# Hybrid trunk on one core: late transfers planned to land later, and a retry, in the kernel's own orderer

## The chip, the cores and the metric

The kernel runs on one core of a Trainium2 chip. The time is the device time of one execution in microseconds; the runs of before gave 1721.27, 1724.09 and 1725.7, median 1724.09. The engines are PE (TensorE; PEld its weight loads), DVE (VectorE), ACT (ScalarE), POOL (GpSimd) and SP (SyncE). Each takes its instructions in the order of its own queue and waits on semaphores. DMA transfers are issued by SP (all loads of weights and tiles, and the last outputs) and by POOL (most stores).

## What is computed

One layer of a hybrid trunk for two request groups, 1024 prompt tokens and 8 x 16 sample tokens, with shared weights, all in float32. Cut to what matters:

```python
mod = silu(c) @ w_ada + b_ada
shift, scale, gate = split(mod[:, None, :], 3)
h = rms_norm(x, norm_g) * (1 + scale) + shift
q, k, v, z_att, z_ssd, xbc, dt_raw, gates = split(h @ w_in, IN_SPLITS)
q, k = rms_norm(q, q_norm_g), rms_norm(k, k_norm_g)          # per head
o_att, k_st, v_st = attn_fn(q, k, v)                          # own chunk + 8 chunks before
att_branch = (o_att * silu(z_att)) @ w_att_proj
xbc, conv_new = causal_dwconv(xbc, conv_buf, conv_w, conv_b)
xs, bm, cm = split(silu(xbc))
dt, a = softplus(dt_raw + dt_bias), -exp(a_log)
y, h_new = ssd_scan(xs, dt, a, bm, cm, h0)                    # chunked scan of 32 heads
y = rms_norm((y + d_skip * xs) * silu(z_ssd), ssd_norm_g)     # in 4 groups
ssd_branch = y @ w_ssd_proj
g_att, g_ssd = split(gates)
out = x + gate * ((sigmoid(g_att) * att_branch + sigmoid(g_ssd) * ssd_branch) @ w_out)
```

D_MODEL is 1024, there are 16 attention heads of 64, the SSD width is 2048 with a state of 128, and 1152 = 1024 + 128 tokens go through the dense layers together. Outputs are `out` and the new keys, values, convolution rows and scan states of both groups.

## The kernel before

`trunk_kernel` lays the work out feature-major: a tile holds 128 features by 1152 tokens (`NT`), in one SBUF area (`arena`, with slots per stage). A dense product in float32 is made of three float16 products: each weight block and operand is split into a high and a low part, and PE adds high x high, high x low and low x high in PSUM (L970, L971, L973 in `dense`, on 384 tokens at a time; L876, L877, L878 in `quad_dense`, on 288).

*Stages.* Attention of the eight head pairs comes first (to about 600 us of the trace). Then come the 16 pairs of SSD heads: a `dense` product for z (evicted at L1985 and L1986), convolution and scan (`ssd`, L2013 and L2113 among its lines, its result written to `y_d` in DRAM), with gate columns in between (`gate_dense`, evicted by ACT's tanh at L1919 and stored by POOL at L1920). From about 1300 us on come the quarter-product stages, all through `quad_dense`: the rest of the gates, the attention projection, the two halves of the SSD projection and the output projection. There a block product is done with seven quarter products instead of eight, from sums and differences of quarters. The sums of the weights are made on DVE by `quad_sums` in the SSD stage and written to `sum_d` in DRAM (POOL, L712), and loaded again later.

*Weights.* `w_ahead` (L679, SP) loads raw weights up to three buffers ahead. `w_split` or `quad_split` splits them: L697 on ACT makes the high part, L698 on DVE the low part; L689 on ACT takes the sum of squares of weights (1024 or 512 wide) and of operands (576 wide) that a later test of the ranges needs.

*Operands of the quarter products.* `differences` (L2209 to L2212, DVE) and `halved` (L2198 ACT, L2200 DVE) split them, `h_pieces` (L2245) and `ssd_prep` (L2281 loads `y_d`, L2286 scales it) feed them. Both are waited for by PE.

*Evictions in `quad_dense`.* `kept` copies the first of a pair of PSUM banks to SBUF (L895, ACT), `joined` adds a second one on DVE (L901). PSUM has three banks of a kind "d", three of a kind "g" and one double one of a kind "s" (the names of PE's outputs begin with these letters), so the eviction of one product frees the bank of a later one. L1108 are four small products for the modulation, which read what L2381 (`mod_gate`, ACT) copied out of PSUM.

*The order.* The program is first recorded in an order in which the generators of the stages take turns. Then `Order` makes the order of every queue anew. `build` forms units: an instruction each, but on PE up to three matmuls of one kind and one output together ("packed"), and any number of small ones; it finds what depends on what by the regions that are read and written, and by the PSUM banks. `run` is a list scheduler with a model of the durations (`cost`): it takes the engine that can go on first, and on it, of the units that are ready by its clock, the earliest in recorded order, with units first whose inputs are there with a margin (`SAFE`: 1000 ns behind PE, 300 behind DVE and ACT, 2500 behind a DMA). The margin decides only among units that are ready; a unit is ready when its inputs' planned ends have passed. For a DMA the planned end comes from eight lanes and one shared bus in `run`. `apply` then chains each engine's instructions in the planned order. Nothing is planned at run time; the real waits are semaphores.

If a test at the end finds a value out of range, a second block of the program (`general_kernel`) computes all again; with these inputs it doesn't run.

## Time and profile before

| | before |
|---|---|
| runs, us | 1721.27, 1724.09, 1725.7; median 1724.09 |
| profiled execution, us | 1723.17 |
| its span, first to last instruction, us | 1721.4 |
| mean granted TensorE clock | 0.998 |
| PE idle from 0 to 600 us, us | 13.18 |
| PE idle from 600 to 1300 us, us | 9.46 |
| PE idle from 1300 to 1700 us, us | 13.52 |
| PE idle from 1700 us to the end, us | 6.64 |

How to read the rows below. In the table of busy times, the number behind the engine is its busy time in microseconds, its share of the span, and the count of instructions. A row of the waits names the waiting engine with its output and line, then the engine, tile and line that ended the wait, then the total, the times and the longest. A row of a timeline has the start and the length in microseconds, the engine, line and operation, what it writes and reads, and in square brackets how long the engine had been idle and who ended that. Matmuls are pipelined: one of 384 columns lasts about 0.33 us, and the next starts about 0.16 us behind it. A row of a chain has the start, the length and what it is. A row of stretches has the stretch, its length, the busy time of PE, PEld, DVE, ACT and POOL with the number of instructions, the granted clock, the share of the DMA engines and GB/s.

### The profile page before, as it was taken

The page shows a single profiled execution, that of the slowest core. Times are in us where ns is not written, and L with a number is a line of the kernel's source. Part 1 is how long each engine was busy: PE and PEld are TensorE (multiplying, and loading weights), DVE is VectorE, ACT ScalarE, POOL GpSimd, SP SyncE. Part 2 cuts the span into 40 slices and gives each one's busy share as a digit, 9 for nine tenths or more (in the row PEclk, how much of TensorE's full clock was granted, in tenths as well). Part 3 has the DMA queues.
Part 4 walks back from the last instruction along what each step waited for, and adds up shares of the span by engine and source line. Part 5 has one row for each costly group of instructions (what it writes and reads, how often), then busy time and mean ns, then how long its engine had stood idle before and what let it go on. Part 6 is the DMA issues. An engine that isn't in the chain of part 4 may idle for free. (4 is left out here: it accounts for less than half of the span.)

```text
span 1721.4 us, 36659 instructions
## 1 busy us (share of the span) xinstructions
PE 1678.6 (98%) x14265; PEld 1120.4 (65%) x14265; DVE 1376.6 (80%) x2539; ACT 1058.1 (61%) x2123; POOL 369.1 (21%) x640
## 2 busy tenths in 40 slices
PE   7999999999999999999999999999999999999998
PEld 3556565556565556666666666666657777777776
DVE  6458767878877888889988998997798677888973
ACT  8766556566565668457655765665379665774550
POOL 0133233135133111322321232232212101010000
PEclk9999999999999999999999999999999999999999
DMA  9248789797978687676858867788756866687661
GB/s 383 82 122 210 170 228 225 168 232 187 219 219 192 165 199 221 181 221 199 194 172 263 241 194 238 235 216 268 284 198 221 274 240 234 232 287 264 224 212 65
DMA packets 299249, 369.16 MB, mean 214 GB/s; under 512 B 211692, under 2 KB 213368, under 8 KB 299064
## 3 DMA queue, kind: packets, MB, share of 16 engines
q1 hardware_dynamic: 282040, 307.65, 64.0%
q0 software_dynamic: 17024, 59.06, 9.3%
q8 instruction: 114, 1.87, 0.5%
q14 instruction: 71, 0.58, 0.1%
HBM read 244.08 MB, written 74.06 MB: 185 GB/s over the span
## 5 line engine op out<-in xcount | busy, mean ns | idle before, releaser
L970 PE MATMUL d<-arena 128*128 128x384 f16 x1320 | 432.0, 327 | 4.4 <-DVE arena L1986 2.0
L973 PE MATMUL d<-arena 128*128 128x384 f16 x1320 | 431.5, 327 | 1.2 <-DVE arena L698 1.2
L971 PE MATMUL d<-arena 128*128 128x384 f16 x1320 | 431.3, 327 | 0.0
L689 ACT ACTIVATE arena<-arena 128x1024 bf16<-128x1024 f32 (+4 forms) x217 | 199.2, 918 | 130.1 <-DMA arena<-in_wall_dram 88.2
L698 DVE SCALAR_TENSOR_TENSOR arena<-arena 128x1024 f16<-128x1024 f32 (+2 forms) x157 | 181.8, 1166 | 61.0 <-ACT arena L697 60.5
L697 ACT ACTIVATE arena<-arena 128x1024 f16<-128x1024 f32 (+2 forms) x157 | 155.4, 994 | 83.2 <-DMA arena<-sum_d 40.5
L970 PEld LDWEIGHTS <-arena 128*128 128x128 f16 x1320 | 129.2, 98 | 90.9 <-issue 12.1
L1023 PE MATMUL d<-arena 128*128 128x384 f16 (+1 forms) x568 | 187.0, 329 | 0.0
L1024 PE MATMUL d<-arena 128*128 128x384 f16 (+1 forms) x568 | 186.3, 328 | 0.0
L1025 PE MATMUL d<-arena 128*128 128x384 f16 (+1 forms) x568 | 186.2, 328 | 0.0
L973 PEld LDWEIGHTS <-arena 128*128 128x128 f16 x1320 | 129.0, 98 | 87.8 <-DVE arena L698 1.9
L971 PEld LDWEIGHTS <-arena 128*128 128x128 f16 x1320 | 129.1, 98 | 82.5 <-issue 5.8
L1569 ACT ACTIVATE arena<-arena 128x640 f32<-128x640 f32 (+4 forms) x144 | 100.8, 701 | 63.4 <-DVE arena L1572 63.0
L877 PEld LDWEIGHTS <-arena 128*128 128x128 f16 x1120 | 109.3, 98 | 39.7 <-issue 12.2
L878 PEld LDWEIGHTS <-arena 128*128 128x128 f16 x1120 | 109.3, 98 | 32.4 <-issue 4.3
L876 PEld LDWEIGHTS <-arena 128*128 128x128 f16 x1120 | 109.4, 98 | 29.3 <-issue 1.5
L876 PE MATMUL d<-arena 128*128 128x288 f16 x400 | 114.5, 286 | 5.9 <-DVE arena L901 3.9
L876 PE MATMUL g<-arena 128*128 128x288 f16 x400 | 114.5, 286 | 1.2 <-DVE arena L901 1.2
L877 PE MATMUL g<-arena 128*128 128x288 f16 x400 | 114.5, 286 | 1.2 <-DVE arena L2200 1.2
L877 PE MATMUL d<-arena 128*128 128x288 f16 x400 | 114.5, 286 | 0.2 <-DVE arena L2200 0.2
L878 PE MATMUL g<-arena 128*128 128x288 f16 x400 | 114.5, 286 | 0.0
L878 PE MATMUL d<-arena 128*128 128x288 f16 x400 | 114.5, 286 | 0.0
(277 smaller groups left out, 3521.8 us busy)
## 6 DMA issues: line engine op xcount, KB each, us to landing
arena<-in_quad_dram SPq DMA_DIRECT2D x80, 512.0 KB, 7.0
arena<-in_wall_dram SPq DMA_DIRECT2D x77, 512.0 KB, 5.2
sum_d<-arena POOLq DMA_DIRECT2D x40, 512.0 KB, 4.9
arena<-sum_d SPq DMA_DIRECT2D x40, 512.0 KB, 4.9
arena<-acs_d SPq DMA_DIRECT2D x32, 576.0 KB, 6.2
arena<-in_kc_dram SPq DMA_DIRECT2D x64, 256.0 KB, 4.4
arena<-in_vc_dram SPq DMA_DIRECT2D x64, 256.0 KB, 3.6
arena<-in_wada_dram SPq DMA_DIRECT2D x24, 512.0 KB, 3.7
```

The source lines that it names most:

```text
L689: keep(nc.scalar.activation(junk[:, :n], x, AF.Square, scale=scale * n ** -0.5, accum_out=sums[:, c:c + 1]))
L697: keep(nc.scalar.activation(hi, x, AF.Copy, scale=scale))
L698: keep(nc.vector.scalar_tensor_tensor(lo, x, scale, hi, ALU.mult, ALU.subtract))
L876: nc.tensor.matmul(ps, wh, xh[:, c], start=first and k == 0, stop=False, skip_group_check=not first)
L877: nc.tensor.matmul(ps, wh, xl[:, c], start=False, stop=False, skip_group_check=not first)
L878: nc.tensor.matmul(ps, wl, xh[:, c], start=False, stop=k == 3, skip_group_check=not first)
L970: nc.tensor.matmul(ps, hi.r[:, wc], kh.r[:, tok], start=k == 0, stop=False)
L971: nc.tensor.matmul(ps, hi.r[:, wc], kl.r[:, tok], start=False, stop=False)
L973: nc.tensor.matmul(ps, lo.r[:, wc], kh.r[:, tok], start=False, stop=k == nk - 1)
L1023: nc.tensor.matmul(ps, kh.r[:, tok], wh, start=k == 0, stop=False)
L1024: nc.tensor.matmul(ps, kh.r[:, tok], wl, start=False, stop=False)
L1025: nc.tensor.matmul(ps, kl.r[:, tok], wh, start=False, stop=k == KT - 1)
```

## The change

Two things. First, if `run` finds no unit that can go on, it no longer stops with an error: it raises `Stuck` with the names of the matmuls that are ready, these are put into a set `apart`, and `build` and `run` are done again with each of them opening a unit of its own. Second, in `run`, a DMA whose planned start is behind 600,000 ns of the planner's clock counts as landed 1000 ns later for everything that reads it. The lanes and the bus go on as before.

```diff
+class Stuck(Exception):
+    pass
...
-        self.pinned, self.cuts = pinned, cuts
+        self.pinned, self.cuts, self.apart = pinned, cuts, set()
...
-                if last and last["key"] == key and x.name not in self.cuts and (small or len(last["ins"]) < 3):
+                if last and last["key"] == key and x.name not in self.cuts and x.name not in self.apart and (small or len(last["ins"]) < 3):
...
-            assert best, ("no unit can go on", [(e, [(u["i"], u["ins"][0].name) for u in ready[e]][:4]) for e in engines])
+            if not best:
+                raise Stuck([x.name for u in ready["PE"] for x in u["ins"]])
...
                 lanes[e][k] = bus + 700
-                lat = bus + 700 - t
+                lat = bus + 700 - t + (1000.0 if t > 600000.0 else 0.0)
...
     order = Order(tc, list(nc.cur_bb.bb.instructions), pinned, cuts, slow, fill, fast)
-    order.build()
-    order.run()
+    while True:
+        order.build()
+        try:
+            order.run()
+            break
+        except Stuck as x:
+            assert not order.apart.issuperset(x.args[0]), "no unit can go on"
+            order.apart.update(x.args[0])
     order.apply()
```

In the built program `apart` stays empty, so the units are those of before. The order is not. It is the same up to about 603 us of the trace of before, and from there on rows change places on all five queues. Three places follow; the lines of the changed kernel are five higher (L1919 is L1924, and so on), and the number behind a name is that of the buffer.

The first is POOL and ACT where the last sum of weights (`sum19_d`) is stored and the modulation is taken out of PSUM (`g664`), from 1244 to 1264 us of the trace. POOL before:

```order
L1920 DMA gate_d_79<-arena_73 128x384
L712 DMA sum19_d_101<-arena_73 256x1x512
L2074 DMA out_hp_dram<-arena_73 128x128
L712 DMA sum19_d_101<-arena_73 256x1x512
L1920 DMA gate_d_79<-arena_73 128x384 x3
L2125 DMA y_d_76<-arena_73 128x1152
```

and now:

```order
L1925 DMA gate_d_79<-arena_73 128x384
L717 DMA sum19_d_101<-arena_73 256x1x512
L2079 DMA out_hp_dram<-arena_73 128x128
L1925 DMA gate_d_79<-arena_73 128x384
L717 DMA sum19_d_101<-arena_73 256x1x512
L1925 DMA gate_d_79<-arena_73 128x384
L2130 DMA y_d_76<-arena_73 128x1152
```

One gate store has moved ahead of the second sum store. ACT at the same time, before:

```order
L1919 ACTIVATE arena_73<-d656_14235 128x384
L689 ACTIVATE arena_73<-arena_73 128x576 x2
L2198 ACTIVATE arena_73<-arena_73 128x1152
L1919 ACTIVATE arena_73<-d660_14325 128x384
L697 ACTIVATE arena_73<-arena_73 128x1024
L2198 ACTIVATE arena_73<-arena_73 128x1152
L689 ACTIVATE arena_73<-arena_73 128x576 x4
L2381 ACTIVATE arena_73<-g664_14407 128x512
```

and now:

```order
L1924 ACTIVATE arena_73<-d656_14235 128x384
L1924 ACTIVATE arena_73<-d660_14325 128x384
L702 ACTIVATE arena_73<-arena_73 128x1024
L694 ACTIVATE arena_73<-arena_73 128x576 x2
L2131 ACTIVATE arena_73<-arena_73 128x1152
L2203 ACTIVATE arena_73<-arena_73 128x1152
L2386 ACTIVATE arena_73<-g664_14407 128x512
L1924 ACTIVATE arena_73<-d663_14371 128x384
L2203 ACTIVATE arena_73<-arena_73 128x1152
L694 ACTIVATE arena_73<-arena_73 128x576 x4
```

An eviction and a weight split have moved ahead of the first two L689, and L2381 ahead of one L2198 and four L689; one L2126 has come forward.

The second is PE, where it reads what L2381 made (`g665`). Before:

```order
L971 MATMUL d666_14428<-arena_73 128x384
L973 LDWEIGHTS arena_73
L973 MATMUL d666_14428<-arena_73 128x384
L1108 MATMUL g665_14408<-arena_73 128x9 x4
L970 LDWEIGHTS arena_73
L970 MATMUL d667_14472<-arena_73 128x384
```

and now:

```order
L976 MATMUL d666_14428<-arena_73 128x384
L978 LDWEIGHTS arena_73
L978 MATMUL d666_14428<-arena_73 128x384
L1113 MATMUL g665_14408<-arena_73 128x9 x4
L975 LDWEIGHTS arena_73
L975 MATMUL d666_14428<-arena_73 128x384
```

The four L1108 stood behind the last of the matmuls of `d666`; now twelve matmuls of `d666` stand behind them.

The third is ACT from 1521 to 1530 us, in the SSD projection, around the evictions of `d739` to `g742`. Before:

```order
L697 ACTIVATE arena_73<-arena_73 128x512
L2198 ACTIVATE arena_73<-arena_73 128x1152
L697 ACTIVATE arena_73<-arena_73 128x1024 x2
L689 ACTIVATE arena_73<-arena_73 128x1024
L895 ACTIVATE arena_73<-d739_17160 128x288
L895 ACTIVATE arena_73<-d740_17161 128x288
L689 ACTIVATE arena_73<-arena_73 128x1024
L895 ACTIVATE arena_73<-g741_17162 128x288
L895 ACTIVATE arena_73<-g742_17163 128x288
```

and now:

```order
L2203 ACTIVATE arena_73<-arena_73 128x1152 x2
L900 ACTIVATE arena_73<-d739_17160 128x288
L900 ACTIVATE arena_73<-d740_17161 128x288
L702 ACTIVATE arena_73<-arena_73 128x512
L702 ACTIVATE arena_73<-arena_73 128x1024
L900 ACTIVATE arena_73<-g741_17162 128x288
L900 ACTIVATE arena_73<-g742_17163 128x288
L702 ACTIVATE arena_73<-arena_73 128x1024
L694 ACTIVATE arena_73<-arena_73 128x1024 x2
```

The evictions of `d739` and `d740` have moved ahead of three weight splits, those of `g741` and `g742` ahead of one split and two L689.

## The prediction

> **What bounds the kernel now.** I read the page's busy table first, then the busy time of the engines by stretch, then the waits of PE behind 600 us, then the timeline of PE at each wait and of the engine that it waits for. Line numbers are those of before; in the changed kernel a line of `trunk_kernel` stands five higher.

> ```profile
> span 1721.4 us, 36659 instructions
> PE 1678.6 (98%) x14265; PEld 1120.4 (65%) x14265; DVE 1376.6 (80%) x2539; ACT 1058.1 (61%) x2123; POOL 369.1 (21%) x640
> ```

> PE is busy nearly throughout, so an order of the same instructions can win only what PE waits. How much of that lies where the order changes (from 603 us on) is read from the stretches. The second column is the length, the third PE's busy time, then PE weight loads, DVE, ACT, POOL.

> ```profile
> 600.00:1300.00 700.00, 690.54 (x5480) 455.47 (x5478) 617.72 (x974) 433.90 (x809) 169.85 (x276) 1.00 0.75 219
> 1300.00:1700.00 400.00, 386.48 (x3137) 305.82 (x3136) 313.23 (x440) 248.21 (x446) 28.35 (x53) 1.00 0.69 235
> ```

> PE's idle time is 9.46 us in the first stretch and 13.52 us in the second: 22.98 us, 1.3% of the span, is all that can be won by ending waits. The waits by who ends them (total, times, longest) show many short ones and one of 3.1 us:

> ```profile
> PE d L876 <- DVE arena L901: 3.9, 4, 1.5
> PE g L1108 <- ACT arena L2381: 3.1, 1, 3.1
> PE d L970 <- DVE arena L1986: 2.0, 1, 2.0
> PE d L973 <- DVE arena L698: 1.2, 2, 0.7
> ```

> The producers are PSUM evictions and small results (L901, L895, L1919, L2381, L2198/L2200). In the timelines below they are ready in time, but stand on ACT or DVE behind an instruction that waits for a DMA. Those queues go in order, so a late transfer holds back work that has nothing to do with it.

> **The change, part by part.** *The taking apart:* in the built program no unit is taken apart; the orderer finds an order at the first try. It costs and gives nothing. *The added microsecond:* no instruction is added or removed. What waits for a transfer is planned 1 us later, so other work is put ahead of it. Counted in the two orders, 594 of DVE's and 567 of ACT's rows stand elsewhere, nearly always by a few rows. PE's 12,785 matmuls are the same; 1,151 of them move, by 99 places at most. Seven places carry the sum.

> (1) Near 1209 us.

> ```profile
> 1208.46 1.04 ACT L697 ACTIVATE arena<-arena 128x1024 f16<-128x1024 f32 x1
> 1209.93 0.32 PE L970 MATMUL d<-arena 128*128 128x384 f16 x1 [1.03 <-ACT arena L1919]
> ```

> PE waits 1.03 us for an eviction that ACT runs behind a weight split of 1.04 us. Now the eviction stands first: **0.95 us** won (0.9 to 1.03).

> (2) The wait at 1260 us. Times and lengths of the matmuls, the chain, ACT, and POOL with its median store (the last number):

> ```profile
> 1258.69 0.33 PE L970 MATMUL d<-arena 128*128 128x384 f16 x1
> ...
> 1260.48 0.33 PE L973 MATMUL d<-arena 128*128 128x384 f16 x1
> 1263.88 1.06 PE L1108 MATMUL g<-arena 128*128 128x9 f32 x8 [3.08 <-ACT arena L2381]
> ...
> 1265.13 0.53 PE L973 MATMUL d<-arena 128*128 128x384 f16 x1
> ...
> 1268.33 0.42 PE L970 MATMUL d<-arena 128*128 128x384 f16 x1
> ```
> ```profile
> 1244.98 7.54 DMA sum_d<-arena
> ...
> 1252.62 1.36 DVE arena L2245
> ```
> ```profile
> 1247.02 0.47 ACT L1919 ACTIVATE arena<-d 128x384 f32<-128x384 f32 x1
> 1254.06 0.69 ACT L689 ACTIVATE arena<-arena 128x576 bf16<-128x576 f32 x1 [6.56 <-issue]
> ...
> 1255.55 1.15 ACT L2198 ACTIVATE arena<-arena 128x1152 f16<-128x1152 f32 x1
> ...
> 1263.25 0.58 ACT L2381 ACTIVATE arena<-g 128x512 f32<-128x512 f32 x1
> ```
> ```profile
> 1247.79 0.56 POOL L1920 DMA_DIRECT2D gate_d<-arena  x1 [2.09 <-ACT arena L1919]
> ```
> ```profile
> sum_d<-arena POOLq DMA_DIRECT2D x40, 512.0 KB, 4.9
> ```

> The second sum store took 7.54 us; DVE's L2245 waited for it, ACT's L689 for L2245, and L2381 came out behind that backlog at 1263.83. Two things move. POOL now issues a gate store ahead of the sum store, and that gate store waits for ACT's L1919, which ends at 1247.49; so the sum store goes out where that issue of 0.56 us ends, near 1248.4, and lands 4.9 (the median row) to 7.54 us later, at 1253.3 to 1255.9. And ACT runs L1919 and L697 in its idle 6.56 us, then two L689, one L2126, one L2198 and L2381, the other L2198 and four L689 behind it. Counted from the landing: L2245 1.36, two L689 1.49 (from 1254.06 to the next row's 1255.55), L2126 and L2198 1.1 each, L2381 0.58, together 5.6: L2381 ends at 1258.9 to 1261.5. But PE has its four L1108 (eight records) twelve matmuls earlier, from 1258.69 on instead of 1260.64. The wait becomes 0.2 to 2.8 us: 0.3 to 2.9 won, and I take **1.5**, the middle, since nothing says which store length comes.

> Behind that wait the matmuls start 0.32 us apart instead of 0.16: from 1265.13 to 1268.33 ten take 3.20 us where the same spacing as at 1258.69 to 1260.48 (1.79 us for eleven) gives 1.63, and the clock says the same:

> ```profile
> 1265.00:1268.60 3.60, 3.60 (x14) 1.75 (x13) 3.60 (x5) 3.60 (x6) 0.58 (x2) 0.53 0.84 267
> ...
> 900.00:903.00 3.00, 1.87 (x11) 0.96 (x11) 3.00 (x4) 0.00 (x0) 0.00 (x0) 1.00 1.07 317
> ```

> 3.60 x (1 - 0.53) = **1.7 us** lost. The second row is behind the 2.0 us wait for L1986, and there the clock stays at 1.00. So the point lies between 2.0 and 3.08 us, and a wait of 1.6 spares the loss (0 to 1.7). [...]

> (3) Near 1370 and 1389 us.

> ```profile
> 1364.74 2.03 DVE L2200 SCALAR_TENSOR_TENSOR arena<-arena 128x576 f16<-128x576 f32 x2 [2.05 <-ACT arena L2198]
> ...
> 1369.54 0.69 DVE L698 SCALAR_TENSOR_TENSOR arena<-arena 128x512 f16<-128x512 f32 x1
> ```
> ```profile
> 1370.64 0.28 PE L876 MATMUL d<-arena 128*128 128x288 f16 x1 [1.53 <-DVE arena L901]
> ```
> ```profile
> 1385.10 4.08 DVE L2286 SCALAR_TENSOR_TENSOR arena<-arena 128x1152 f32<-128x1152 f32 x3
> ```
> ```profile
> 1389.59 0.28 PE L876 MATMUL d<-arena 128*128 128x288 f16 x1 [0.78 <-DVE arena L901]
> ```

> At the first, the wide L2200 (2.03 less about 0.7 for the narrow one, 1.3) now goes into DVE's idle 2.05 us and the L698 (0.6 of its 0.69) goes behind L901: L901 is 1.9 us earlier, the 1.53 is gone: **1.5** (0.9 to 1.5). At the second, L901 now stands ahead of the three L2286, 4.08 us: **0.8** (0.4 to 0.8).

> (4) From 1460 to 1480 us.

> ```profile
> 1459.32 1.06 ACT L697 ACTIVATE arena<-arena 128x1024 f16<-128x1024 f32 x1 [7.90 <-DMA arena<-sum_d]
> ```
> ```profile
> 1462.47 0.28 PE L876 MATMUL s<-arena 128*128 128x288 f16 x1 [1.43 <-ACT arena L2198]
> 1463.27 0.28 PE L877 MATMUL s<-arena 128*128 128x288 f16 x1 [0.51 <-DVE arena L2200]
> ...
> 1472.02 0.28 PE L877 MATMUL g<-arena 128*128 128x288 f16 x1 [1.17 <-DVE arena L2200]
> ```

> ACT idles 7.90 us for a loaded sum, with two L689 and the L2198 that PE needs behind it; now these go first and 1.94 us of waits end. The DVE chain that ends at 1472.02 begins with another load and doesn't move, so an earlier PE waits longer there: of 3.11 us in all I count **1.7** (0.8 to 2.6).

> (5) From 1527 to 1546 us.

> ```profile
> 1523.99 1.06 ACT L697 ACTIVATE arena<-arena 128x1024 f16<-128x1024 f32 x1 [1.32 <-DMA arena<-sum_d]
> 1526.15 1.06 ACT L697 ACTIVATE arena<-arena 128x1024 f16<-128x1024 f32 x1 [1.11 <-DMA arena<-in_quad_dram]
> ```
> ```profile
> 1528.60 0.28 PE L876 MATMUL d<-arena 128*128 128x288 f16 x1 [1.34 <-ACT arena L895]
> ...
> 1543.07 0.28 PE L876 MATMUL g<-arena 128*128 128x288 f16 x1 [1.08 <-DVE arena L901]
> 1545.73 0.28 PE L876 MATMUL d<-arena 128*128 128x288 f16 x1 [1.40 <-DVE arena L901]
> ```

> ACT's L895 now stand ahead of those two splits, over 4 us earlier, and DVE's L901 ahead of a wide L2200. Of 3.82 us I count **2.0** (1.2 to 3.8): a PE that is 1.3 us earlier asks for the next ones sooner too.

> *What it costs.* Weight splits (L697, L698, L689) and what is issued for them on SP stand one to six microseconds later; their cover is that a split is mostly done long before PE takes the weights: PE waited for L698 1.2 us in all. If the cover is gone, each costs what it is late. PE work that is pulled ahead can also meet producers that didn't move. The trace has no row for such waits; the bounds are 0 and as much as 0.43 (the share of DVE and ACT rows behind 600 us that move, 1,161 of 2,669) of the 22.98 us, 10 us, if moved rows are waited for as often as before. I take **3**, nearer to nothing, since what moves up is what PE waited for and what moves back is mostly not.

> Sum: 0.95 + 1.5 + 1.7 + 1.5 + 0.8 + 1.7 + 2.0 = 10.15 won, less 3, is 7.15 (lower ends 4.5 with nothing for the clock, upper ends 14.3). The profiled execution took 1723.17 us, 0.92 below the median of 1724.09: 1716.0 on its own count, **1716.9** against the median.

> **The rivals.**

> *No change.* What PE wins it gives back at the next wait that belongs to a chain of its own.

> ```profile
> 1636.91 0.28 PE L877 MATMUL s<-arena 128*128 128x288 f16 x1 [1.60 <-DVE arena L2200]
> ```

> DVE's order ahead of this one is as it was; DVE is busy 313 of 400 us between 1300 and 1700, and 618 of 700 before. If it is DVE's chain that sets the pace there, only the lower ends count, less the 3: 4.5 - 3 = 1.5, 1722.6 us. For it: DVE's L2200 ends several waits. Against it: DVE idles by itself behind ACT, 2.05 us at 1364.74.

> *Slower: the splits come too late.* Weights are split in pairs by ACT and DVE, and in the quarter-product stages from 1300 us on they now stand behind evictions. Each one moved behind one more L697 is 1.06 us later. Once more than ten of them are late by that much (10.15 / 1.06), the gain is gone; with fifteen it is 15.9 - 10.15 = 5.8 us slower, 1729.9. For it: two waits for L698 are there now already. Against it: the longest is 0.7 us.

> *The half clock stays*, since the wait falls only to its upper end, or since the clock falls for another reason than the wait: 1.7 less of gain, 5.45 won, 1718.6. The 1.00 behind 2.0 us and the 0.53 behind 3.08 speak against it. [...]

> *The change doesn't do what it says*: for the taking apart that is so already, and it is in the sum at nothing.

> **How the numbers follow.** My forecast, 1711 to 1718.8, has 0.45; the half clock that stays 0.08; no change or nearly so 0.33; slower 0.14. About 0.3% (5.2 us) is what a measurement of this kernel can tell from no change: faster is below 1718.9, slower above 1729.3. So faster 0.53, same 0.33, slower 0.14. The range goes from the upper ends of the gains less the 3 (1724.09 - 11.3 = 1712.8), lowered to 1709.8 where the new waits come to nothing (14.3 won), up past no change to 1727; beyond it lies the slower rival and little else.

> **What would show it.** PE's idle time between 600 and 1700 us falls from 22.98 to about 17.5; L1108 waits under 2 us and the clock behind it stays at 1.00; the waits for L1919 near 1209, for L901 near 1370 and 1389 and for L895 near 1528 are gone. Wrong would be: new waits for L698, L697 or a load among PE's waits, above 3 us together; or the same places, with PE earlier and the wait longer by as much.

## The result, and the profile after

The changed kernel takes 1710.83 us (median of 6 runs, 1708.03 to 1711.62), the kernel before 1723.76 in the same comparison (1720.77 to 1725.7). The ratio is 0.9926, 95% interval 0.9913 to 0.9938: 12.9 us or 0.74% faster, where 7.2 us had been forecast. The first rows of the page, and the stretches (length, PE, PEld, DVE, ACT, POOL, clock, DMA share, GB/s), of the changed kernel:

```profile
span 1709.0 us, 36656 instructions
PE 1674.9 (98%) x14265; PEld 1121.9 (66%) x14265; DVE 1376.4 (81%) x2539; ACT 1061.6 (62%) x2123; POOL 389.5 (23%) x640
```
```profile
600.00:1300.00 700.00, 692.95 (x5515) 458.98 (x5514) 621.11 (x979) 438.30 (x811) 192.14 (x280) 1.00 0.75 220
1300.00:1700.00 400.00, 393.06 (x3200) 312.82 (x3198) 315.70 (x455) 248.14 (x445) 26.27 (x49) 1.00 0.68 235
1264.00:1268.00 4.00, 4.00 (x30) 2.19 (x29) 4.00 (x11) 3.94 (x8) 0.25 (x1) 1.00 0.55 166
```

PE does the same 14,265 records. Its idle time between 600 and 1700 us fell from 22.98 to 7.05 + 6.94 = 13.99 us, and its busy time by 3.7 us, of which the half clock behind the wait of L1108 is one part: at 1264 us the clock is now 1.00. The waits that are left have other places than before:

```profile
PE d L975 <- ACT arena L1809: 3.3, 3, 1.7
PE s L881 <- ACT arena L900: 3.0, 2, 1.6
PE d L975 <- DVE arena L1991: 2.2, 2, 1.7
PE d L881 <- DVE arena L906: 1.8, 3, 1.3
```

Where the time went is seen best by following the same matmul through both traces. Start in the changed kernel less start before, as a median over each stretch of 20 us of the trace of before (the whole execution runs 0.36 us later from its first loads on); only the steps over 0.5 us are listed, and one at the edge of a stretch can belong to its neighbour:

```
us of before    step, us     us of before    step, us
860             +0.97        1160            -0.67
900             -2.97        1200            -1.23
940             -0.54        1260            -5.02
960             +1.04        1360            -2.01
980             +1.52        1400            -0.73
1000            +0.67        1460            -1.04
1060            +1.83        1520            -1.50
1140            -0.88        1540            -1.30
                             1640            -0.74
at 1220: +1.01               at 1700: -11.91
```

Up to 1220 us gains and losses cancel (+0.65 beside the 0.36); from 1260 us on every listed step is a gain, most of them at the places that were named. The largest is the wait for L2381 (now L2386). ACT, the sum store (in the table of DMA issues from 1243 to 1260 us), and PE in the changed kernel:

```profile
1252.14 0.49 ACT L1924 ACTIVATE arena<-d 128x384 f32<-128x384 f32 x1 [5.02 <-PE d L978]
1252.53 1.05 ACT L702 ACTIVATE arena<-arena 128x1024 f16<-128x1024 f32 x1
1254.32 0.68 ACT L694 ACTIVATE arena<-arena 128x576 bf16<-128x576 f32 x1 [0.74 <-DVE arena L2250]
...
1257.92 0.57 ACT L2386 ACTIVATE arena<-g 128x512 f32<-128x512 f32 x1
```
```profile
sum_d<-arena POOLq DMA_DIRECT2D x1, 512.0 KB, 3.3
```
```profile
1259.70 0.95 PE L1113 MATMUL g<-arena 128*128 128x9 f32 x8
```

L2386 ends at 1258.49 and PE comes at 1259.70: the row has no bracket, so nothing is waited for. The sum store, issued behind the gate store as expected, took 3.3 us. Of the 5.02 us, 3.35 are won at the wait and 1.67 over the matmuls right behind it, where the clock had been half.

### The profile page after: what moved, and what is told of

It is laid out like the page before. It is cut to its first block, busy times and chain, and to the rows that moved or that the text cites. A ratio compares the mean times of both kernels' runs of the same rounds, so it can differ in the third digit from the quotient of the medians.

```text
span 1709.0 us, 36656 instructions
## 1 busy us (share of the span) xinstructions
PE 1674.9 (98%) x14265; PEld 1121.9 (66%) x14265; DVE 1376.4 (81%) x2539; ACT 1061.6 (62%) x2123; POOL 389.5 (23%) x640
## 3 DMA queue, kind: packets, MB, share of 16 engines
q8 instruction: 114, 1.87, 0.5%
## 5 line engine op out<-in xcount | busy, mean ns | idle before, releaser
L694 ACT ACTIVATE arena<-arena 128x1024 bf16<-128x1024 f32 (+4 forms) x217 | 199.1, 917 | 74.0 <-DMA arena<-in_wall_dram 43.5
## 6 DMA issues: line engine op xcount, KB each, us to landing
arena<-in_quad_dram SPq DMA_DIRECT2D x80, 512.0 KB, 6.4
arena<-in_wall_dram SPq DMA_DIRECT2D x77, 512.0 KB, 5.0
sum_d<-arena POOLq DMA_DIRECT2D x40, 512.0 KB, 5.5
arena<-sum_d SPq DMA_DIRECT2D x40, 512.0 KB, 4.6
arena<-in_wada_dram SPq DMA_DIRECT2D x24, 512.0 KB, 4.2
```

The source lines that it names most:

```text
L694: keep(nc.scalar.activation(junk[:, :n], x, AF.Square, scale=scale * n ** -0.5, accum_out=sums[:, c:c + 1]))
```

## The experiments

Each run is compared with runs of before on the same chip, so the ratios are what counts; the medians of before there were 1724.55 to 1725.57.

### Is it the margin, or a lucky draw of the order?

One number was changed, five times:

```diff
-                lat = bus + 700 - t + (1000.0 if t > 600000.0 else 0.0)
+                lat = bus + 700 - t + (-700.0 if t > 600000.0 else 0.0)
...
+                lat = bus + 700 - t + (300.0 if t > 600000.0 else 0.0)
...
+                lat = bus + 700 - t + (700.0 if t > 600000.0 else 0.0)
...
+                lat = bus + 700 - t + (1500.0 if t > 600000.0 else 0.0)
...
+                lat = bus + 700 - t + (2000.0 if t > 600000.0 else 0.0)
```

> Transfers behind 600,000 ns are planned to land 700 ns earlier instead of 1000 ns later: 542 of DVE's rows stand elsewhere, about as many as in the changed kernel. Theory (the direction matters, since the order now puts still more behind transfers that aren't there yet): PE idles more between 600 and 1700 us than the 23.0 us of before, 26 to 36, and the time is 1727 to 1737. Rival (any new draw of the order is worth the same, and the 12.7 us were luck): as likely faster as slower, within 1717 to 1731, with a mean at no change; or, if before was an unlucky draw, near 1714.

> 300 ns instead of 1000 for all transfers planned behind 600,000 ns. Theory (the margin itself is what helps, by keeping PE's producers out from behind late transfers, so more margin up to the real lateness is better): part of the gain, 1716 to 1722, between 0 and 1000 ns. Rival (the direction matters little near zero and each number draws another order, worth plus or minus 10 us): anything from 1712 to 1735, with no trend over 300, 700, 1500 and 2000.

> 700 ns instead of 1000. Theory: close to the changed kernel, 1711 to 1717. Rival (a draw): anything from 1712 to 1735, no trend.

> 1500 ns instead of 1000. Theory: as good as 1000 ns or better, 1706 to 1714. Rival (a draw): anything from 1712 to 1735, no trend.

> 2000 ns instead of 1000. Theory: the waits for transfers get rarer still, but weight splits and loads come later, since each load waits for a buffer that a delayed split frees; no further gain, 1708 to 1722. Rival (a draw): anything from 1712 to 1735, no trend.

| added to a late transfer, ns | ratio to before | 95% interval | this median, us |
|---|---|---|---|
| -700 | 1.0229 | 1.0189 to 1.0268 | 1762.23 |
| 0 (the retry alone, see below) | 0.9994 | 0.9975 to 1.0014 | 1722.38 |
| 300 | 0.9971 | 0.9946 to 0.9995 | 1719.28 |
| 700 | 0.9932 | 0.9908 to 0.9955 | 1712.86 |
| 1000 (the change) | 0.9926 | 0.9913 to 0.9938 | 1710.83 |
| 1500 | 0.9969 | 0.9944 to 0.9993 | 1717.58 |
| 2000 | 1.0044 | 1.0023 to 1.0064 | 1732.78 |

The seven points fall once and rise once, with the lowest part near 700 to 1000 ns, which the intervals don't tell apart. Of the 5040 orders in which seven values can stand, 64 do that, so seven independent draws would rarely look like this: that each number only draws another order is very unlikely. The theory missed the size at both ends. At 1500 and 2000 ns it expected too much (1706 to 1714, and 1708 to 1722): the far side of the curve rises sooner. At -700 ns it expected 1727 to 1737 with 26 to 36 us of idle time on PE between 600 and 1700 us, and the run took 1762 with 55.3. Both ends can be read in the profiles. PE's waits with -700 ns, and ACT and DVE at the longest of them:

```profile
PE d L975 <- DVE arena L1991: 15.0, 7, 6.6
```
```profile
867.83 1.28 ACT L2018 ACTIVATE arena<-arena 128x128 f32<-128x128 f32 x4 [13.41 <-DMA arena<-acs_d]
869.01 1.17 ACT L1834 ACTIVATE arena<-arena 128x1176 f32<-128x1176 f32 x1
870.09 0.47 ACT L1990 ACTIVATE arena<-d 128x384 f32<-128x384 f32 x1
```
```profile
870.21 1.23 DVE L1838 SCALAR_TENSOR_TENSOR arena<-arena 128x1024 f32<-128x1024 f32 x1 [11.08 <-ACT arena L1834]
...
871.56 0.55 DVE L1991 SCALAR_TENSOR_TENSOR arena<-arena,d 128x384 f32<-128x384 f32 x1
```

ACT stood 13.41 us at an L2018 that wanted a load of `acs_d`, with an eviction (L1990) queued behind it; DVE stood 11.08 us behind ACT, and PE 6.57 us behind both. This is the mechanism at its plainest. The changed kernel shows the other side of it. At 1018 us its ACT stands 7.79 us for such a load, but here the eviction (the first row) came ahead of the row that waits for the load, and PE's longest wait there is 0.78 us:

```profile
1009.55 0.49 ACT L1990 ACTIVATE arena<-d 128x384 f32<-128x384 f32 x1 [3.41 <-PE d L978]
...
1018.77 0.40 ACT L2018 ACTIVATE arena<-arena 128x128 f32<-128x128 f32 x1 [7.79 <-DMA arena<-acs_d]
```

With 2000 ns the waits are others:

```profile
PE g L881 <- ACT arena L702: 10.5, 1, 10.5
PE g L883 <- DVE arena L703: 6.5, 1, 6.5
```
```profile
1293.04 1.15 ACT L2203 ACTIVATE arena<-arena 128x1152 f16<-128x1152 f32 x1
1294.09 1.04 ACT L702 ACTIVATE arena<-arena 128x1024 f16<-128x1024 f32 x1
1295.04 1.15 ACT L2203 ACTIVATE arena<-arena 128x1152 f16<-128x1152 f32 x1
```
```profile
1295.19 0.42 PE L881 MATMUL g<-arena 128*128 128x288 f16 x1 [10.49 <-ACT arena L702]
1302.36 0.42 PE L883 MATMUL g<-arena 128*128 128x288 f16 x1 [6.51 <-DVE arena L703]
```

Now it is the weight split itself that comes too late. ACT isn't idle before it (no bracket): it does other work that this order puts ahead. That the later planned load is the reason is argued from the change, not read from the trace. PE waits 17.0 us for the two halves of one weight, and from 1288 to 1308 us, with the clock at 0.50 nearly throughout, it is busy for 6.3 us; half of that, about another 3 us, is an estimate of what the half clock costs. Until there this order stood as well as the change: its matmuls near 1270 us start 6.35 us before those of the first trace of before.

### Does the retry do anything, and what belongs to one execution only?

```diff
-                lat = bus + 700 - t + (1000.0 if t > 600000.0 else 0.0)
+                lat = bus + 700 - t + 0.0
```

> The retry alone, without the added microsecond: the order of every queue is that of before, row for row. All theories: no change, 1724. Its profile is a second look at the order of before: waits that show in the first profile and not in this one belong to one execution, not to the order. From the runs so far I expect the 2.0 us wait near 898 us (gone in all four) and the one near 1209 us to be missing here too, and the 3.1 us wait of L1113 to be shorter than 3 us if the second sum store takes less than 7.5 us.

The ratio is 0.9994 (0.9975 to 1.0014): no change. Its trace shows a second execution of the order of before (PE's waits, its timeline near 900 us, the clock behind it):

```profile
PE g L1113 <- ACT arena L2386: 2.7, 1, 2.7
PE d L978 <- DVE arena L703: 1.3, 2, 0.7
PE d L975 <- DVE arena L1991: 1.2, 1, 1.2
```
```profile
901.09 0.32 PE L975 MATMUL d<-arena 128*128 128x384 f16 x1 [1.18 <-DVE arena L1991]
902.23 0.34 PE L978 MATMUL d<-arena 128*128 128x384 f16 x1 [0.65 <-DVE arena L703]
```
```profile
904.00:906.00 2.00, 2.00 (x8) 0.91 (x6) 1.14 (x2) 2.00 (x3) 0.00 (x0) 0.50 1.14 311
```

The wait near 1209 us isn't there, though the rows that were blamed stand as before. But it is there in the run `late` of the next section, which has the order of before up to 1230 us, and it is 1.31 us long. So this order has the wait in some executions only:

```profile
1212.59 0.32 PE L975 MATMUL d<-arena 128*128 128x384 f16 x1 [1.31 <-ACT arena L1924]
```

The wait near 898 us is shorter, not gone, with a half clock behind it, so that expectation held in part. The second sum store took 7.26 us and L1113 waited 2.7, as expected. The waits near 1260, 1370 and 1389 us are there again (no step above 0.4 us at these places). PE idles 18.89 us between 600 and 1700 us here, against 22.98 in the first trace, and has three half-clock stretches there instead of one (mean granted clock 0.996 against 0.998 over the whole trace); the two executions take the same time (1723.09 and 1723.17). So the idle time of one trace isn't the order's alone.

### Where does the gain arise?

```diff
-                lat = bus + 700 - t + (1000.0 if t > 600000.0 else 0.0)
+                lat = bus + 700 - t + (1000.0 if 600000.0 < t < 1210000.0 else 0.0)
...
+                lat = bus + 700 - t + (1000.0 if t > 1210000.0 else 0.0)
```

> The added microsecond is given only to transfers planned between 600,000 and 1,210,000 ns: the order is that of the changed kernel up to about 1245 us of the trace of before, and from there nearly that of before. Theory (the gain is made behind 1245 us, where evictions and small results no longer stand behind instructions that wait for transfers): PE's matmuls near 1220 us stand 0.65 us later than before, as in the changed kernel, the 3.1 us wait of L1113 and the half clock behind it stay, and the time is 1724 to 1725, no change. Rival (the gain is the sum of many small shifts from 600 us on, and the place matters little): about half of the 12.7 us, near 1717.

> The added microsecond is given only to transfers planned behind 1,210,000 ns: the order of before up to about 1230 us, and from there row for row that of the changed kernel. Theory: the whole gain and a little more, since the small losses between 600 and 1100 us are left out: 12.3 + 0.65 = 12.9 us less, near 1711. Rival (many small shifts everywhere): about half of the gain, near 1717.

The second (`late`) gives 0.9926 (0.9899 to 0.9953): all of the gain, with the order of before up to 1230 us. The first (`mid`) gives 0.9963 (0.9942 to 0.9983), which isn't the "no change" that was expected: about 6.4 us. Its trace says why: ACT's rows near 1255 us are not those of the changed kernel, but here too L2386 stands ahead of the L2203 and the four L694 that held it up, so the wait near 1260 us is gone (the step there is -5.02, too). At 1220 us this run's matmuls stand 0.80 us later than before, so what lies ahead of 1245 us gives nothing. The gain is thus made from 1245 us on, 5.0 us of it at the modulation.

The rest can't be credited to the moved rows place by place. From 1357 us of the trace of before on, the rows of all five engines stand in `mid` in the same order as before, and yet its trace has steps of -2.01 near 1370, -1.10 near 1460 and -1.50 near 1528 us, much as in the changed kernel. Near 1370 and 1528 us the waits of 1.53 and 1.34 us are gone or below 0.4 us in the two runs with moved rows as well (below), again without the rows that the prediction names there. What comes only with the changed order is what lies next to them: near 1389 us `mid` waits 1.67 us, near 1543 us 0.85 us, and in the changed kernel PE waits at neither:

```profile
1384.04 0.28 PE L881 MATMUL d<-arena 128*128 128x288 f16 x1 [1.67 <-DVE arena L906]
```

Why the waits near 1370 and 1528 us go without their rows isn't settled.

### Loads or stores?

```diff
-                lat = bus + 700 - t + (1000.0 if t > 600000.0 else 0.0)
+                lat = bus + 700 - t + (1000.0 if t > 600000.0 and e == "SP" else 0.0)
...
+                lat = bus + 700 - t + (1000.0 if t > 600000.0 and e == "Pool" else 0.0)
```

> The added microsecond only for the transfers that SP issues (loads). Theory (the gain comes from rows that no longer stand behind instructions waiting for loads of weights, sums and y_d): most of the gain, 1711 to 1715. Rival (the gain comes from POOL's stores, whose landing frees buffers and so releases the operand chain at 1250 us): under 5 us, 1719 or more.

> The added microsecond only for the transfers that POOL issues (stores). Theory (loads matter): 0 to 5 us less, 1719 to 1724. Rival (stores matter): 1711 to 1715.

Loads alone give 0.9953 (0.9927 to 0.9979), about two thirds of the gain and a little short of what was expected. Stores alone are slower, 1.0094 (1.0066 to 1.0122), which neither theory had. The largest loss in that trace is again behind a row that waits for a load:

```profile
1025.35 0.69 ACT L2018 ACTIVATE arena<-arena 128x128 f32<-128x128 f32 x2 [14.48 <-DMA arena<-acs_d]
```
```profile
PE d L975 <- DVE arena L1991: 9.3, 3, 7.1
```

The parts don't add up (-0.47% and +0.94% against -0.74% together): an order made anew isn't a sum. Why stores alone lose in the other places wasn't settled.

### Would one moved row do?

In the order of before, without any margin, L2386 was put ahead of the rows that held it up; then the second modulation's as well:

```diff
+    q = order.order["Activation"]
+    at = [u["i"] for u in q]
+    q.insert(at.index(6708), q.pop(at.index(6752)))
...
+    at = [u["i"] for u in q]
+    q.insert(at.index(6842), q.pop(at.index(6870)))
```

> The order of before, with one row moved: L2386 of g664 on ACT now stands ahead of one L2203 and four L694. Theory: L2386 ends near 1258.5 us, PE doesn't wait for it, and the half clock behind the wait is gone: 3.1 + 1.7 = 4.8 us less, near 1719, if nothing behind it takes that back; PE's matmuls near 1300 us start 4.8 us earlier. Rival (DVE sets the pace there, or the half clock comes from something else): 3.1 us at 1270, and up to all of it given back by 1400.

> The order of before with two rows moved on ACT: L2386 of g664 ahead of one L2203 and four L694 as in s_all, and L2386 of g674 ahead of the two L694 before it. Theory (in s_all 4.6 us were won at 1260 us and 3.65 given back at the second modulation, whose L2386 stood behind two L694, 1.5 us): the second wait falls from 1.7 to 0.2 us, there is no half clock behind it, and PE is about 3 us earlier from 1290 us on than in s_all; 1715 to 1717. Rival (DVE sets the pace of that stretch, so the time comes back whatever ACT's order): another wait takes it back before 1320 us, 1719 to 1720 as in s_all.

The first gives 0.9975 (0.9954 to 0.9996). The step near 1260 us is -4.59 (-3.34 at the wait, -1.67 behind it, then +0.43), though the sum store goes out as before and takes 7.13 us: moving L2386 alone ends this wait, with the sum store left where it was. But +3.65 comes back at 1290:

```profile
1283.17 1.06 PE L1113 MATMUL g<-arena 128*128 128x9 f32 x8 [1.72 <-ACT arena L2386]
```
```profile
1284.00:1287.00 3.00, 3.00 (x18) 2.00 (x18) 1.10 (x1) 2.35 (x5) 0.00 (x0) 0.61 0.52 156
```

With the second row moved too, the theory failed: 1.0018 (1.0001 to 1.0034), not faster at all. PE there:

```profile
1288.74 1.06 PE L1113 MATMUL g<-arena 128*128 128x9 f32 x8 [0.85 <-ACT arena L2386]
...
1295.10 0.28 PE L881 MATMUL g<-arena 128*128 128x288 f16 x1 [0.88 <-ACT arena L2203]
...
1296.91 0.28 PE L882 MATMUL g<-arena 128*128 128x288 f16 x1 [1.53 <-DVE arena L2205]
```

The wait of 1.72 is halved, and 2.4 us of waits for the split operands (L2203, L2205) follow a few matmuls later: ACT's and DVE's chain of operands sets the pace between 1280 and 1300 us, as the rival had it. The rival's time, 1719 to 1720, didn't come either: the median is 1726.58. In the trace of this run the matmuls near 1160 us already stand 5.2 us later than in the first trace of before, ahead of any moved row. Most of that, 4.4 us, arises near 1018 us, where ACT waited 9.37 us for a load of `acs_d` (3.25 in the first trace, with the same order of rows), and PE then waited 2.52 us for L1991 (the other 1.9 us isn't traced to a row):

```profile
1014.26 1.28 ACT L2018 ACTIVATE arena<-arena 128x128 f32<-128x128 f32 x4 [9.37 <-DMA arena<-acs_d]
```

So a single execution's time also holds what the order doesn't set. Whether the other nine executions had this loss isn't known, and so why the second moved row made the median worse stays open. What stands: moved by itself, the row that PE waits for brings a gain that the next rows take back in large part, and the changed kernel, where many more rows have moved, keeps it: its PE has no wait above 0.3 us from there to 1350 us.

## Why the prediction was right

The sign and the mechanism held, and most of the named waits are gone; the size was too small (7.2 us forecast, 12.9 measured), by several terms, of which the wait near 1260 us is the largest. By its steps:

- *The taking apart at nothing*: shown by the retry alone, 0.9994.
- *Near 1209 us, 0.95*: the step is -1.23, but the retry alone has it too, with the order of before. The wait is there in two of five executions of these rows (1.03 and 1.31 us), so the term holds what some executions lose, not what the order always does; that its number came out here is partly luck.
- *Near 1260 us, 1.5 + 1.7*: 3.35 + 1.67 = 5.02. The price of the half clock was right, the wait was mis-sized: it went altogether, not by half. The sum store was given 4.9 to 7.5 us behind its gate store, and it took 3.3, less than the range allowed (4.7 in `late`, with the same order; 6.8 to 7.5 in four traces of the order of before). The working from L2245 on was right (5.6 us from there to the end of L2381; 1252.94 to 1258.49 measured).
- *Near 1370 and 1389 us, 2.3*: 2.0 and 0.9, read in steps of 5 us. The reason given for the first, the two moved rows of DVE, isn't shown: three runs without them lose the wait as well. For the second it fits, since those runs keep a wait at 1389 us.
- *1460 to 1480 us, 1.7*: 1.04 and 0.44. The wait near 1472 us stays (1.2 us), as the prediction said, and a new one of 1.6 us stands at 1459.
- *1527 to 1546 us, 2.0*: 2.5 (1.50 and 1.30, less 0.28). Of the three waits named, 1.34 and 1.08 us are gone, and the last, 1.40, is still 1.34. That the moved rows end the first isn't shown, since it goes without them too.
- *New waits, 3 lost*: net +1.9 from 600 to 1180 us (new waits for L1809 and L1991; a shorter wait near 898 us is set against them), and 0.74 won at 1640 us that wasn't counted.

The sum of the steps is -1.2 - 5.0 - 2.9 - 1.5 - 2.5 + 1.9 - 0.7 = -11.9 within rounding and the small steps, against -12.3 read directly (11.91 + 0.36).

Of the rivals, "the splits come too late" is what happens at 2000 ns, with 17.0 us in one place, where the prediction had set many small delays. "What PE wins it gives back" is what happens to a single moved row, for the most part. At 1000 ns the change sits between the two. "The half clock stays" didn't occur; but the bound that the prediction drew for it, a length of the wait between 2.0 and 3.08 us, was the wrong kind of bound, as the last section shows.

## What to carry to other kernels

In this kernel, where the engines took their instructions in order, a late transfer cost most where a result that the bottleneck waits for stood behind its consumer in another engine's queue: 13.41 us of ACT's waiting for `acs_d` came with 6.57 us of PE's at -700 ns, while 7.79 us in the changed kernel, with the eviction ahead, came with 0.78 at most. Look for rows of idle time "<-DMA" on an engine that isn't the bottleneck, and at what is queued behind them. In a list scheduler with fixed durations a pessimistic landing time moves all such rows at once, and here there was a best size: measure a few on both sides of zero, since too little left the bottleneck behind loads, and too much left the weights behind other work. Don't read a wait in one trace as the order's own before a second execution shows it too, and don't credit its end to the rows beside it before a run with those rows unmoved has kept it.

## What the runs showed of the hardware that was not expected

The half clock does not need a wait near 3 us. It came behind 1.72 us in the run with one moved row and behind 1.18 and 0.65 us, half a microsecond apart, in the retry alone, but not behind 1.67 us in the changed kernel:

```profile
1054.42 0.32 PE L975 MATMUL d<-arena 128*128 128x384 f16 x1 [1.67 <-DVE arena L1991]
```
```profile
1054.50:1058.00 3.50, 3.50 (x23) 2.07 (x23) 2.86 (x3) 3.47 (x5) 0.25 (x1) 1.00 1.24 277
```

```profile
1281.24:1284.65 3.41, 1.70 (x15) 1.38 (x14) 3.31 (x4) 2.25 (x7) 0.54 (x1) 1.00 0.98 398
1284.65:1288.06 3.41, 3.41 (x16) 2.08 (x15) 1.33 (x4) 3.38 (x6) 0.00 (x0) 0.50 0.58 177
```
```profile
1017.19:1020.60 3.41, 1.51 (x12) 1.21 (x11) 0.00 (x0) 1.81 (x5) 0.00 (x0) 1.00 1.03 415
1020.60:1024.01 3.41, 2.47 (x18) 1.92 (x18) 0.00 (x0) 3.38 (x9) 0.00 (x0) 1.00 0.92 352
```

The 2.0 us wait of before near 900 us was split likewise (PE idles 1.37 and 1.26 us in the two windows), so its 1.00 set no lower bound. Why the band from 1.5 to 1.95 us goes both ways isn't shown.

Such a stretch cost 1.67 us near 1265 us (the same matmuls in the changed kernel and in the run with one moved row; 1.7 was worked out), and a trace of the order of before showed one in one execution and three in another before the tail; the changed kernel's showed none. That may be a part of the spread of before (1716.2 to 1736.3 over the chips), but no run here separates it from the transfers' own.
